# An attention and mLSTM kernel: the mLSTM chunks shared out over twelve attention items, queries split in the projection, output weights in another load order

## The chip, the cores and the metric

The kernel runs on one core of one Trainium2 chip. The metric is the device time of one execution in microseconds (us). A core has five engines that work in parallel: PE (matrix products), DVE (vector), ACT (scalar functions), POOL (a second, slower vector engine) and SP, whose queue here issues the DMA transfers. Each engine runs its own queue in order and waits for others through semaphores.

## The reference

One layer on 1024 tokens of width 1024, with 256 context tokens. One input projection feeds two head groups side by side; their outputs are concatenated, projected by w_out, and a feed-forward part follows.

```python
px = modulate(rms_norm(x, g_pre_mix), sh_m, sc_m) @ w_in
aq, ak, av, mq, mk, mv, mo, mg = split(px)
# 8 query heads on 2 key heads of 64, window 128, all 256 context keys, one sink logit per head
att = window_attention(rope(aq), rope(ak), av, kc, vc, attn_sink)
# 4 heads, keys of 64, values of 128, forward and backward scan, summed
h   = mlstm_bidir(mq, mk, mv, gates, state_f, state_b)
ml  = rms_norm(h) * gain * sigmoid(mo)
x   = x + gt_m * rms_norm(concat(att, ml) @ w_out)
x   = x + gt_f * rms_norm(swiglu(modulate(rms_norm(x), ...)))
```

Everything is float32. Where PE multiplies, an operand is split into a rounded part h and a remainder l (h by an ACT cast or a POOL multiplication, l by a subtraction), and products are summed from the parts: two for the scores (`qh`, `ql`), three for weights (`mm3`).

## The kernel before

The program goes through these stages, each with the time at which it stands in the profiled execution: modulation vectors and the token preparation (to about 150); the transposed projections (to 308), one tile of 128 output columns after the other in the order of `TILES`; attention with mLSTM (309 to 488); the output projection, the norms and the feed-forward part (to 1245). The change touches the second and third.

*Projection.* Each of the four query tiles `aq0` to `aq3` holds two heads. `rope` (L466-475) rotates the tile in the SBUF buffer `T(0)`, and two DMAs store it to the DRAM tensor `aq_d` (L616). After `aq3` come the tiles `mo0` to `mo3`, the sigmoid output gates (`so`, L620). Beside them the mLSTM queries are weighted: `ml_queries` loads weights into `qb` (L577), POOL multiplies (L580), and a store puts them into `q_dr` (L581).

*Attention.* There are 16 items, one per block of 128 queries and key group: item i is block i // 2, group i % 2, four heads. For an item `q_load` (L561) fetches `qd` from `aq_d`, and `q_split` makes `qh` and `ql` on POOL (L567, L568). `Soft` computes the scores of a head on PE (L774, L775: four matmuls in inner blocks, "one head" below), adds mask and minimum on DVE (L776), takes the exponential on ACT (L785) and normalizes on POOL (L790). `Values` transposes the probabilities on PE (`tr`, L804, "T"), splits them on ACT and DVE (L59, L60: `th`, `tl`), multiplies with the values (`mm`, L814, L815, "M") and combines the heads (`out`, L822, L823). Item i does its own values and the scores of item i + 2.

*mLSTM.* There are eight chunks n of 128 tokens, both directions. `ml_load` fetches weights `wl`, queries `qp` and gates `hs`; `ml_scores` (PE L689) puts scores into one of the two PSUM buffers called `s`, which the attention scores use too, and DVE multiplies them into `wl` (L694, four instructions); `ml_values` is called for four quarters of a chunk (PE L703, L704; DVE L707-709, L715; ACT L713); `ml_norm` squares on ACT (L722-724) and scales on POOL (L725); `ml_out` transposes on PE (L731, "z" with the chunk's number: z6 is the output of chunk 6) and multiplies with the gate on DVE (L732). Chunk i goes with item i, items 0 to 7; its output is taken one item later.

*Output weights.* `wout_load(j)` fetches 128 rows of w_out as `wor` (L744), casts to `woh` on ACT (L745) and subtracts to `wol` on POOL (L746); one j goes through half-wide loads with an ACT cast and a DVE subtraction instead (`load_split`). The three buffers are SBUF slots `R(k)`, shared in time with `wl`, `qp` and `hs`: a slot is written when its last reader is done. It runs in items 9 to 13.

*Order.* The instructions of a stage are put into their queues by a scheduler that works from the order in which the code calls them; `PLAN_ML` and `PLAN` are strings of operations that set this order for an item (T, M, O values; A scores and N norm of the item two ahead; q split; V, x, s, z, w mLSTM; l weights). The last two items, with the first block's output projection (`omm`: PE L71-73 on `woh`, `wol` and the split `mix`), are written out by hand behind `tc.manual_schedule()`.

Of the kernel before, what the change touches and what calls it, by code (L numbers as in the profile page):

```python
# [9 lines left out]
F32 = mybir.dt.float32  # L10
F32R = mybir.dt.float32r
# [20 lines left out]
VSIL, VCONV, VGML, VBADA, VGPM, VGPF = 0, 16, 28, 32, 64, 72  # L32
NVEC = 80
RW = 1032
PLAN_ML = "T0 q A0 A1 A2 A3 T1 T2 T3 M0 M1 T4 V0 N0 M2 V1 M3 M4 O z V2 w V3 s N1 x"
PLAN = "T0 q A0 A1 A2 A3 T1 T2 T3 N0 M0 T4 M1 M2 N1 M3 M4 O z l"


def body(tc, x, ctx, vecs, bcv, bada, gqm, gqf, wada, ws1, ws2, wt, wout, wfi, wfo,
# [45 lines left out]
    c = cp[1]  # L85
# [324 lines left out]
    dma(cost, cosc)  # L410
    dma(sint, sinc)
    so_d = tc.dram_tile([4, P, S], F32, name="so_d")
    aq_d = tc.dram_tile([8, 64, S], F32, name="aq_d")

    def T(i, name):
        return q2.tile([P, S], F32, name=name, tag=f"s{i}")
# [146 lines left out]
    def q_split(i):
        qd = qds.pop(i)
        qh = qq.tile([P, 4, P], F32R, name="qh", tag="qh", bufs=2)
        ql = qq.tile([P, 4, P], F32R, name="ql", tag="ql", bufs=2)
        pool.tensor_scalar(qh, qd, 1.0, 1.0, MUL, MUL)  # L567
        pool.tensor_tensor(ql, qd, qh.bitcast(F32), SUB)  # L568
        qhl[i] = qh, ql

    def ml_queries(d, j):

# [13 lines left out]
    for j, name in enumerate(TILES):  # L586
        if j + 1 < len(TILES):
            tload(j + 1)
        if name in rest2:
            ada_rest2(rest2[name])  # L590
        ps = tproj(j, name in ("mk0", "mk1", "ak"))
        i = int(name[-1]) if name[-1].isdigit() else 0
        if name.startswith("mk"):
            conv(ps, convw[:, 2 + i], (mk[i], mkc[:, i]), 1.0)
        elif name.startswith("mq"):
            conv(ps, convw[:, i], (mq[i],), 0.125)
        elif name == "ak":
            kr, ks = R(6, "kr", (S,)), R(7, "ks", (S,))
            rope(ps, kr, 1.0)
            kc = q2.tile([P, S + 2], F32, name="kc", tag="cr")  # L600
            act.copy(kc[:, 0:L], ps[2][:, :L])
            th = T(0, "kth")
            for a, b, w, dst in ((kr, ks, S, slice(0, S)), (kc[:, 0:L], kc[:, L:2 * L], L, slice(S, S + L))):
                t = th[64:P] if w == S else kc[64:P, 2 * L:3 * L]
                dma(b[0:64], a[64:P])
                dma(b[64:P], a[0:64])
                for g in range(2):
                    act.copy(k2[g][0:64, dst], (b if g else a)[0:64])
                    lo = (a if g else b)[64:P]
                    act.copy(t.bitcast(F32R), lo)  # L610
                    dve.tensor_tensor(k2[g][64:P, dst], lo, t, SUB)
        elif name.startswith("aq"):
            t = T(0, f"aq{i}")
            rope(ps, t, 0.125)
            for g in range(2):
                dma(aq_d[4 * g + i], t[64 * g:64 * g + 64])  # L616
        else:
            t = R(14 if i == 3 else 15, "so", (S,))
            for k in range(2):
                act.activation(t[:, k * 512:(k + 1) * 512], ps[k], AF.Sigmoid)  # L620
            dve.tensor_scalar(t, t, vec[:, VGML + i:VGML + 1 + i], None, MUL)
            dma(so_d[i], t)
        if name in rest:
            ada_rest(rest[name], j + 1)
        if name == "aq3":
            close(p2)
            aqp = open_pool("attq")
            qq = aqp[1]
            for i in range(2):
                q_load(i)  # L630
                q_split(i)
# [37 lines left out]
    wts, qps, hss = {}, {}, {}  # L669

    def ml_load(n):
        wts[n] = R((10, 12, 14)[n % 3], f"wl{n}", (2, 4, P))
        dma(wts[n].rearrange("p d h t -> p (d h t)"), w_dr[n])
        qps[n] = R((13, 15)[n % 2], f"qp{n}", (2, 2, P))
        for d in range(2):
            m = 7 - n if d else n
            dma(qps[n][:, d], q_dr[d, :, :, m * P:(m + 1) * P].rearrange("j p t -> p j t"))
        t = R((9, 11)[n % 2], f"hs{n}", (2, 4, P))
        dma(t[:, 1], so_d[:, :, n * P:(n + 1) * P].rearrange("h p t -> p h t"))
        hss[n] = t[:, 0], t[:, 1]  # L680
# [51 lines left out]
        dve.tensor_tensor(mix[n][:, 4:8, :], pt, so, MUL)  # L732

    def wout_load(j):
        h, l = R(2 * j, f"woh{j}", (D,), F32R), R(2 * j + 1, f"wol{j}", (D,), F32R)
        if j == 0:
            for i in range(2):
                sl = slice(i * 512, (i + 1) * 512)
                load_split(h[:, sl], l[:, sl], wout[j][:, sl],
                           qq.tile([P, 4, P], F32, name="wor0", tag="qd", bufs=2).rearrange("p a b -> p (a b)"))  # L740
            wo[j] = h, l
            return
        raw = R(2 * j - 1, f"wor{j}", (D,))
        dma(raw, wout[j])  # L744
        act.copy(h, raw)  # L745
        pool.tensor_tensor(l, raw, h.bitcast(F32), SUB)  # L746
# [77 lines left out]

    tc.keep_in_program_order(act.preload_act_table_set("natural_log_exp_and_others"))
    ml_load(0)
    for i in range(2):
        a = Soft(i)
        for h in range(4):
            a.scores(h)  # L830
            if h % 2:
                a.norm(h // 2)
        if i == 0:
            q_load(2)
            ml_scores(0)

    for i in range(NIT):
        a = Soft(i + 2) if i + 2 < NIT else None
# [2 lines left out]
            q_load(i + 3)  # L841
        if i == NIT - 2:
            break
        for k in (PLAN_ML if i < NT else PLAN).split():
            op, n = k[0], int(k[1:] or 0)
            if op == "q" and a:
                q_split(i + 2)
            elif op == "w" and i + 1 < NT:
                ml_load(i + 1)
            elif op == "T" and n < b.nt:  # L850
                b.tr(n)
            elif op == "M" and n < b.nt:
                b.mm(n)
            elif op == "O":
                b.out()
            elif op == "A" and a:
                a.scores(n)
            elif op == "N" and a:
                a.norm(n)
            elif op == "V" and i < NT:  # L860
                ml_values(i, n // 2, n % 2)
            elif op == "x" and i < NT:
                ml_norm(i)
            elif op == "s" and i + 1 < NT:
                ml_scores(i + 1)
            elif op == "z" and 1 <= i <= NT:
                ml_out(i - 1)
            elif op == "l" and i > NT:
                for j in {9: (7,), 10: (6,), 11: (5, 4), 12: (3, 2), 13: (1, 0)}[i]:
                    wout_load(j)  # L870
# [5 lines left out]
    mhl = {}  # L876

    def msplit(n, hf):
        h, l = (qq.tile([P, 4, P], F32R, name=f"m{x_}{hf}", tag=f"q{x_}", bufs=2) for x_ in "hl")
        split(h, l, mix[n][:, 4 * hf:4 * hf + 4, :])  # L880
        mhl[n, hf] = h, l

    def omm(n, hf, ks):
        h, l = mhl[n, hf]
        for k in ks:
            j = 4 * hf + k
            for i in range(2):
# [6 lines left out]

    b.tr(0)
    b.tr(1)
    msplit(0, 1)
    b.tr(2)
    omm(0, 1, range(1))
    mm_t(b, 0, 1)  # L900
    b.tr(3)
    omm(0, 1, range(1, 2))
    mm_t(b, 2, 3)
    b2 = Values(NIT - 1)
    b2.tr(0)
# [12 lines left out]
    close(atp)
    close(aqp)
# [787 lines left out]
```

## Time and profile before

| | us |
|---|---|
| median of 3 runs | 1248.03 (1245.07 to 1248.34) |
| profiled execution | 1247.24 |
| its span | 1245.4 |
| PE busy in the span | 1205.8 |
| DVE / ACT / POOL busy | 799.9 / 580.1 / 204.0 |

The granted TensorE clock is at its full value nearly throughout. In the page's fourth part, the chain that ended last, a step "DVE" or "DMA" means that the work behind it waited for that engine. The rows that matter for the change are those of the stage from 309 to 488.

### The profile page before, as it was taken

How to read it: one execution, taken by the hardware profiler on the slowest of the kernel's cores; microseconds unless marked ns; L12 is line 12 of the kernel's file. 1: busy time of each engine (PE TensorE's matmuls, PEld its weight loads, DVE VectorE, ACT ScalarE, POOL GpSimd, SP SyncE). 2: the span in 40 equal slices, each digit the busy share in tenths (PEclk: the TensorE clock that was granted, in tenths of full speed). 3: DMA queues.
4: the chain of work that ended last, by engine and by line, in shares of the span. 5: the costliest groups of instructions: out<-in, count | busy, mean ns of one | idle time of the engine just before them, and what ended most of it. 6: DMA issues, size and time to landing. Idle time of an engine off the chain costs nothing.

```text
span 1245.4 us, 16232 instructions
## 1 busy us (share of the span) xinstructions
PE 1205.8 (97%) x5859; PEld 971.7 (78%) x5859; DVE 799.9 (64%) x1375; ACT 580.1 (47%) x1111; POOL 204.0 (16%) x245
## 2 busy tenths in 40 slices
PE   7889999999999998999899999999999999999997
PEld 1779887877777786888678888888888878888885
DVE  3882268763877787355867677767776655554566
ACT  3754533111666796677633333333333325434542
POOL 0752401244644475000000000000000000000000
PEclk9899999999999999999999999999999999999999
DMA  8532855655422320522033465665644547665853
GB/s 310 173 123 73 300 164 152 186 147 197 121 85 86 114 74 9 203 81 72 17 104 140 162 220 189 216 237 191 216 144 169 180 160 268 203 212 187 308 172 118
DMA packets 90952, 201.78 MB, mean 162 GB/s; under 512 B 9076, under 2 KB 29940, under 8 KB 89464
## 3 DMA queue, kind: packets, MB, share of 16 engines
q1 hardware_dynamic: 90872, 200.74, 48.1%
q8 instruction: 46, 0.75, 0.2%
q14 instruction: 34, 0.28, 0.1%
HBM read 149.32 MB, written 50.73 MB: 161 GB/s over the span
## 4 chain that ended last, share of the span: by engine, by line
PE 74%; DVE 9%; DMA 7%; ACT 4%; POOL 2%; issue 2%; SPq 1%; DVEq 0%; POOLq 0%; ACTq 0%
PE xv L72 7%; PE xv L71 7%; PE xv L73 7%; PE pt L72 5%; PE pt L71 5%; PE pt L73 5%; PE pt L704 2%; PE pt L703 2%; PE pt L804 2%; DMA wb<-in_wada 2%; PE t L438 2%; PE t L441 2%; PE t L439 2%; PE s L774 1%; PE op L71 1%
## 5 line engine op out<-in xcount | busy, mean ns | idle before, releaser
L60 DVE TENSOR_TENSOR fo<-fr,fo 128x1024 fp32r<-128x1024 f32 x77 | 92.7, 1222 | 71.4 <-ACT fo L59 68.4
L59 ACT CAST fo<-fr 128x1024 fp32r<-128x1024 f32 x77 | 79.6, 1051 | 74.0 <-PE pt L73 36.5
L438 PE MATMUL t<-hh,th 128*128 128x512 f32 x208 | 83.4, 401 | 0.9 <-ACT cr L455 0.9
L439 PE MATMUL t<-hl,th 128*128 128x512 f32 x208 | 82.6, 397 | 0.0
L59 ACT CAST wS<-wr 128x512 fp32r<-128x512 f32 x88 | 54.1, 622 | 57.9 <-PE pt L73 38.0
L60 DVE TENSOR_TENSOR wS<-wr,wS 128x512 fp32r<-128x512 f32 x88 | 60.4, 688 | 20.8 <-ACT wS L59 20.7
L71 PE MATMUL xv<-tT,wS 128*128 128x512 f32 x168 | 67.7, 403 | 3.7 <-ACT tT L1079 2.0
L441 PE MATMUL t<-hh,tl 128*128 128x512 f32 x208 | 68.6, 394 | 0.0
L72 PE MATMUL xv<-tT,wS 128*128 128x512 f32 x168 | 67.6, 402 | 0.0
L73 PE MATMUL xv<-tT,wS 128*128 128x512 f32 x168 | 66.6, 397 | 0.3 <-DVE wS L60 0.3
L489 DVE SCALAR_TENSOR_TENSOR acc<-wb,csil,acc 128x1024 f32<-128x1024 f32 x24 | 34.4, 1433 | 39.4 <-DMA wb<-in_wada 39.2
L438 PEld LDWEIGHTS t<-hh,th 128*128 128x128 f32 x208 | 39.1, 188 | 10.1 <-ACT cr L455 1.3
L940 DVE TENSOR_TENSOR wr<-wr 128x512 f32<-128x512 f32 x66 | 45.5, 689 | 1.5
L439 PEld LDWEIGHTS t<-hl,th 128*128 128x128 f32 x208 | 39.1, 188 | 8.4 <-issue 1.2
L1191 ACT ACTIVATE es<-es 128x512 f32<-128x512 f32 x22 | 13.9, 632 | 67.6 <-DVE es L943 67.6
L441 PEld LDWEIGHTS t<-hh,tl 128*128 128x128 f32 x208 | 38.2, 188 | 8.5 <-issue 1.0
L71 PE MATMUL op<-woh,mh 128*128 128x512 f32 x112 | 44.7, 399 | 0.0
L72 PE MATMUL op<-wol,mh 128*128 128x512 f32 x112 | 44.2, 394 | 0.0
L73 PE MATMUL op<-woh,ml 128*128 128x512 f32 x112 | 44.1, 394 | 0.0
L774 PE MATMUL s<-k,qh 128*128 128x256 f32 (+1 forms) x128 | 41.5, 335 | 1.9 <-ACT so L620 1.0
L71 PE MATMUL pt<-fo 128*128 128x512 f32 x110 | 42.8, 389 | 0.0
L72 PE MATMUL pt<-fo 128*128 128x512 f32 x110 | 42.8, 389 | 0.0
(982 smaller groups left out, 3498.1 us busy)
## 6 DMA issues: line engine op xcount, KB each, us to landing
wr<-in_wfi SPq DMA_DIRECT2D x44, 512.0 KB, 5.0
wb<-in_wada SPq DMA_DIRECT2D x24, 512.0 KB, 4.1
s_d<-a SPq DMA_DIRECT2D x22, 512.0 KB, 6.5
bt<-in_wfo SPq DMA_DIRECT2D x44, 256.0 KB, 4.0
tb_d<-bt SPq DMA_DIRECT2D x11, 1024.0 KB, 3.9
fr<-s_d SPq DMA_DIRECT2D x44, 256.0 KB, 3.5
fr<-tb_d SPq DMA_DIRECT2D x44, 256.0 KB, 4.6
fr<-a_d SPq DMA_DIRECT2D x33, 256.0 KB, 4.3
```

What stands on the lines that cost most here:

```text
L59: act.copy(hi, raw)
L60: dve.tensor_tensor(lo, raw, hi.bitcast(F32), SUB)
L71: pe.matmul(ps, a[0], b[0], start=first, stop=False, **kw)
L72: pe.matmul(ps, a[0], b[1], start=False, stop=False, **kw)
L73: pe.matmul(ps, a[1], b[0], start=False, stop=last, **kw)
L438: pe.matmul(o, wh[:, kt], m[0], start=f, stop=False)
L439: pe.matmul(o, wh[:, kt], m[1], start=False, stop=False)
L441: pe.matmul(o, wl[:, kt], m[0], start=False, stop=l)
L489: dve.scalar_tensor_tensor(a, t, csil[:, kt, 0:1], a, MUL, ADD)
L703: pe.matmul(pv[:, j, :], qp_[r, d, j, :], cs[r, j, :], start=True, stop=False)
L774: pe.matmul(o, qh[:, h, :], k2[g][:, kc], start=True, stop=False)
L940: dve.tensor_tensor(out, a, b, SUB)
```

## The change

Three things are done at once.

1. *Queries.* `q_split` is gone. Each `aq` tile is split when it is projected (an ACT cast into slot 3, a DVE subtraction in place, 128 x 1024 each), and both parts are stored, so that `aq_d` becomes two DRAM tensors. The stores go from 8 to 16 (256 KB each) and the query loads of the items from 32 to 64 (128 KB each). The query tiles get three buffers in place of two.
2. *mLSTM.* One `PLAN` serves all items. At five places of an item, `a` to `e`, the table `ML3` names what is done of the mLSTM: three items do two chunks, so that eight chunks take twelve items (0 to 11, and the last output in item 12). In an entry the letter is the step (V values, s scores, x norm, y output, w and h loads), the first digit the chunk, counted from the first of the pair, and V's second digit the quarter. `ml_load` is cut in two.
3. *Output weights.* They are loaded in the order 1, 2, 3, 4, 0, 5, 6, 7 in place of 7, 6, 5, 4, 3, 2, 1, 0, in other slots (`WSLOT`, `WRAW`: the raw rows of 4, 0 and 5 share slot 14), and block 0's output projection begins with the attention half.

```diff
-PLAN_ML = "T0 q A0 A1 A2 A3 T1 T2 T3 M0 M1 T4 V0 N0 M2 V1 M3 M4 O z V2 w V3 s N1 x"
-PLAN = "T0 q A0 A1 A2 A3 T1 T2 T3 N0 M0 T4 M1 M2 N1 M3 M4 O z l"
+PLAN = "A0 A1 A2 A3 T0 T1 T2 T3 M0 M1 T4 a N0 M2 b M3 M4 O c d N1 e"
+ML3 = ({"a": "V00", "b": "V01", "c": "y9", "d": "V02", "e": "s1"},
+       {"a": "V03 x0", "b": "V10", "c": "V11", "d": "y0", "e": "w2 h2"},
+       {"a": "V12", "b": "s2", "c": "V13", "d": "", "e": "x1 w3"})
+WLOADS = {9: (1,), 10: (2, 3), 11: (4,), 12: (0, 5), 13: (6, 7)}
+WSLOT = ((0, 3), (1, 2), (4, 5), (6, 7), (8, 9), (10, 13), (14, 11), (12, 15))
+WRAW = (14, 8, 8, 8, 14, 14, 12, None)
...
-    def q_split(i):
-        qd = qds.pop(i)
-        qh = qq.tile([P, 4, P], F32R, name="qh", tag="qh", bufs=2)
-        ql = qq.tile([P, 4, P], F32R, name="ql", tag="ql", bufs=2)
-        pool.tensor_scalar(qh, qd, 1.0, 1.0, MUL, MUL)
-        pool.tensor_tensor(ql, qd, qh.bitcast(F32), SUB)
-        qhl[i] = qh, ql
+        qhl[i] = [qq.tile([P, 4, P], F32R, name=f"q{p}", tag=f"q{p}", bufs=3) for p in "hl"]
+        for t, src in zip(qhl[i], aq_d):
+            for d in range(2):
+                dma(t[64 * d:64 * d + 64].bitcast(F32), src[4 * g:4 * g + 4, :, n * P:(n + 1) * P].rearrange("h d t -> d h t"))
...
             rope(ps, t, 0.125)
-            for g in range(2):
-                dma(aq_d[4 * g + i], t[64 * g:64 * g + 64])
+            qp2 = R(3, f"aqh{i}", (S,), F32R), t.bitcast(F32R)
+            split(*qp2, t)
+            for d, o in zip(aq_d, qp2):
+                for g in range(2):
+                    dma(d[4 * g + i], o[64 * g:64 * g + 64].bitcast(F32))
...
+    def ml_work(i, k):
+        c0 = i // 3 * 2
+        for w in ML3[i % 3][k].split():
+            op, n, k_ = w[0], c0 + (int(w[1]) if w[1] != "9" else -1), int(w[2:] or 0)
...
-        h, l = R(2 * j, f"woh{j}", (D,), F32R), R(2 * j + 1, f"wol{j}", (D,), F32R)
+        h, l = (R(k, f"wo{p}{j}", (D,), F32R) for k, p in zip(WSLOT[j], "hl"))
...
+            raw = R(WRAW[j], f"wor{j}", (D,))
...
+    OORD = {0: (2, 3, 1, 0, 4, 5, 6, 7)}
```

How this moves instructions, at three places. First SP's queue at the end of the query tiles. Before, in order: the last query tile's stores, the loads of two items, the weights of the mLSTM queries (`qb`), with the third item's loads between.

```order
L616 DMA aq_d<-aq_2272 64x1024 x2
L561 DMA qd<-aq_d 64x4x128 x4
L577 DMA qb_2311<-w_d 64x8x128 x2
L577 DMA qb_2323<-w_d 64x8x128 x2
L561 DMA qd<-aq_d 64x4x128
L622 DMA so_d<-so 128x1024
L561 DMA qd<-aq_d 64x4x128 x3
L581 DMA q_dr<-qb_2311 128x1024
L577 DMA qb_2419<-w_d 64x8x128 x2
L581 DMA q_dr<-qb_2323 128x1024
L577 DMA qb_2514<-w_d 64x8x128 x2
```

The changed order at the same place:

```order
L619 DMA aq_dh<-aqh_2298 64x1024 x2
L619 DMA aq_dl<-aq_2288 64x1024 x2
L569 DMA qh<-aq_dh 64x4x128 x2
L569 DMA ql<-aq_dl 64x4x128 x2
L569 DMA qh<-aq_dh 64x4x128 x2
L569 DMA ql<-aq_dl 64x4x128 x2
L577 DMA qb_2330<-w_d 64x8x128 x2
L577 DMA qb_2342<-w_d 64x8x128 x2
L625 DMA so_d<-so 128x1024
L569 DMA qh<-aq_dh 64x4x128 x2
L569 DMA ql<-aq_dl 64x4x128 x2
L581 DMA q_dr<-qb_2330 128x1024
```

There are two more stores and four more query loads ahead of the first `qb` load.

Second PE's queue where a chunk's scores (`s<-mq,mk`) stand. Before, here the scores of chunk 5 in item 4; `pt<-cst,pr_` are transposes of probabilities:

```order
L704 MATMUL pt<-V,wl_3446 128x129
L689 MATMUL s<-mq_1333,mk_1331 128x128 x2
L689 MATMUL s<-mq_1334,mk_1332 128x128 x2
L774 MATMUL s<-k_0_1324,qh 128x384
L775 MATMUL s<-k_0_1324,ql 128x384
L774 MATMUL s<-k_0_1324,qh 128x256
L775 MATMUL s<-k_0_1324,ql 128x256
L804 MATMUL pt<-cst,pr__3309 128x128 x12
L814 MATMUL po<-th__3683,av_88 128x512
L774 MATMUL s<-k_0_1324,qh 128x384
L775 MATMUL s<-k_0_1324,ql 128x384
```

The changed order, here the scores of chunk 6 in item 8; `pt<-cst,hs_` is the output of chunk 4:

```order
L710 MATMUL pt<-V,wl_3712 128x129
L695 MATMUL s<-mq_1333,mk_1331 128x128 x2
L695 MATMUL s<-mq_1334,mk_1332 128x128 x2
L779 MATMUL s<-k_1_1325,qh 128x384
L780 MATMUL s<-k_1_1325,ql 128x384
L779 MATMUL s<-k_1_1325,qh 128x256
L780 MATMUL s<-k_1_1325,ql 128x256
L779 MATMUL s<-k_1_1325,qh 128x384
L780 MATMUL s<-k_1_1325,ql 128x384
L779 MATMUL s<-k_1_1325,qh 128x256
L780 MATMUL s<-k_1_1325,ql 128x256
L737 MATMUL pt<-cst,hs_3565 128x128 x4
```

The twelve transposes that stood between the first and the second head behind the chunk's scores now stand behind both heads and the output of chunk 4.

Third POOL's queue over the last items. Before (`pr_` are probabilities being normalized, `wol` the weights' remainders, here those of 4, 3, 2 and 1):

```order
L746 TENSOR_TENSOR wol_4635<-wor_4636,woh_4634 128x1024
L790 TENSOR_SCALAR pr__4416<-pr__4416,sm 128x640 x2
L567 TENSOR_SCALAR qh<-qd 128x512
L746 TENSOR_TENSOR wol_4744<-wor_4745,woh_4743 128x1024
L790 TENSOR_SCALAR pr__4525<-pr__4525,sm 128x640 x2
L763 COPY pr__4640<-bcr 128x4
L568 TENSOR_TENSOR ql<-qd,qh 128x512
L790 TENSOR_SCALAR pr__4525<-pr__4525,sm 128x640 x2
L746 TENSOR_TENSOR wol_4750<-wor_4751,woh_4749 128x1024
L763 COPY pr__4755<-bcr 128x4
L790 TENSOR_SCALAR pr__4640<-pr__4640,sm 128x512 x4
L746 TENSOR_TENSOR wol_4856<-wor_4857,woh_4855 128x1024
```

The changed order from the second last chunk output on; `hs_4027` is chunk 6, `hs_4304` chunk 7, and the `wol` are those of 4, 0, 5 and 6:

```order
L731 TENSOR_TENSOR hs_4027<-hs_4027,sq 128x512
L795 TENSOR_SCALAR pr__4502<-pr__4502,sm 128x640 x2
L751 TENSOR_TENSOR wol_4639<-wor_4640,woh_4638 128x1024
L768 COPY pr__4644<-bcr 128x4
L795 TENSOR_SCALAR pr__4644<-pr__4644,sm 128x512 x2
L751 TENSOR_TENSOR wol_4753<-wor_4754,woh_4752 128x1024
L795 TENSOR_SCALAR pr__4644<-pr__4644,sm 128x512 x2
L768 COPY pr__4764<-bcr 128x4
L751 TENSOR_TENSOR wol_4759<-wor_4760,woh_4758 128x1024
L731 TENSOR_TENSOR hs_4304<-hs_4304,sq 128x512
L795 TENSOR_SCALAR pr__4764<-pr__4764,sm 128x512 x4
L751 TENSOR_TENSOR wol_4861<-wor_4862,woh_4860 128x1024
```

The splits (`qh`, `ql`) are gone, and the scaling of chunk 7 stands behind the remainders of weights 4, 0 and 5. On PE the output of chunk 7 stands ahead of all transposes of item 13.

More of the change, by code (lines that the diff above doesn't have):

```diff
@@ L412, in body @@
     so_d = tc.dram_tile([4, P, S], F32, name="so_d")
-    aq_d = tc.dram_tile([8, 64, S], F32, name="aq_d")
+    aq_d = [tc.dram_tile([8, 64, S], F32, name=f"aq_d{p}") for p in "hl"]
     def T(i, name):
@@ L734, in wout_load @@
     def wout_load(j):
-        h, l = R(2 * j, f"woh{j}", (D,), F32R), R(2 * j + 1, f"wol{j}", (D,), F32R)
-        if j == 0:
-            for i in range(2):
+        h, l = (R(k, f"wo{p}{j}", (D,), F32R) for k, p in zip(WSLOT[j], "hl"))
+        if j == 7:
+            for i, p in enumerate("hl"):
                 sl = slice(i * 512, (i + 1) * 512)
                 load_split(h[:, sl], l[:, sl], wout[j][:, sl],
[L740 to L746, printed above, removed]
+                           qq.tile([P, 4, P], F32, name="wor7", tag=f"q{p}", bufs=3).rearrange("p a b -> p (a b)"))
+        else:
+            raw = R(WRAW[j], f"wor{j}", (D,))
+            dma(raw, wout[j])
+            act.copy(h, raw)
+            pool.tensor_tensor(l, raw, h.bitcast(F32), SUB)
         wo[j] = h, l
@@ L835, in body @@
             ml_scores(0)
+            ml_load(1)
+            ml_load2(1)
+    def ml_work(i, k):
+        c0 = i // 3 * 2
+        for w in ML3[i % 3][k].split():
+            op, n, k_ = w[0], c0 + (int(w[1]) if w[1] != "9" else -1), int(w[2:] or 0)
+            if not 0 <= n < NT:
+                continue
+            if op == "V":
+                ml_values(n, k_ // 2, k_ % 2)
+            elif op == "x":
+                ml_norm(n)
+            elif op == "y":
+                ml_out(n)
+                if w[1] == "9" and n + 2 < NT:
+                    ml_load2(n + 2)
+            elif op == "s":
+                ml_scores(n)
+            elif op == "w":
+                ml_load(n)
+            elif op == "h":
+                ml_load2(n)
     for i in range(NIT):
@@ L843, in body @@
             break
-        for k in (PLAN_ML if i < NT else PLAN).split():
+        for k in PLAN.split():
             op, n = k[0], int(k[1:] or 0)
[L846 to L850, printed above, removed]
+            if op == "T" and n < b.nt:
                 b.tr(n)
@@ L859, in body @@
                 a.norm(n)
[L860 to L870, printed above, removed]
+            elif op in "abcde":
+                ml_work(i, op)
+        for j in WLOADS.get(i, ()):
+            wout_load(j)
     order = tc.manual_schedule()
@@ L896, in body @@
     b.tr(1)
-    msplit(0, 1)
+    msplit(0, 0)
     b.tr(2)
-    omm(0, 1, range(1))
+    omm(0, 0, range(1))
     mm_t(b, 0, 1)
     b.tr(3)
-    omm(0, 1, range(1, 2))
+    omm(0, 0, range(1, 2))
     mm_t(b, 2, 3)
```

23 lines of the change are left out of this document (11 added, 12 removed).

## The prediction

> **What bounds the kernel now.** I read the page's shares and its chain first, then the span cut into stretches, then each engine in order of time where PE idles.
>
> ```profile
> PE 1205.8 (97%) x5859; PEld 971.7 (78%) x5859; DVE 799.9 (64%) x1375; ACT 580.1 (47%) x1111; POOL 204.0 (16%) x245
> ...
> PE 74%; DVE 9%; DMA 7%; ACT 4%; POOL 2%; issue 2%; SPq 1%; DVEq 0%; POOLq 0%; ACTq 0%
> ...
> 325.00:440.00 115.00, 113.90 (x675) 89.48 (x675) 86.10 (x282) 76.70 (x217) 54.59 (x71) 1.00 0.33 99
> 440.00:487.00 47.00, 42.19 (x269) 35.04 (x267) 42.69 (x94) 39.73 (x90) 38.36 (x39) 1.00 0.10 30
> ...
> 460.00:470.00 10.00, 9.88 (x67) 8.61 (x66) 9.91 (x25) 8.22 (x18) 10.00 (x11) 1.00 0.09 29
> 470.00:480.00 10.00, 8.61 (x59) 7.06 (x57) 8.52 (x22) 9.54 (x23) 10.00 (x12) 1.00 0.09 26
> 480.00:490.00 10.00, 7.13 (x35) 5.12 (x36) 8.62 (x13) 5.41 (x11) 3.47 (x5) 1.00 0.00 1
> ...
> 485.26 0.50 PE L815 MATMUL po<-tl__4820,av 128*128 128x512 f32 x1 [1.25 <-DVE tl__4820 L60]
> ```
>
> A stretch's row gives its length, then busy time and instructions of PE, its weight loads, DVE, ACT and POOL, then the granted clock; the last row is one instruction: start, duration, and the wait in front of it with its releaser. PE is busy for 97% of the whole. The stage that the change rewrites runs from 309.5 to 487.6, and PE fills its first part too (113.90 of 115). Only items 8 to 15 leave something: 4.81 us idle of 47, while POOL works without a pause (10.00 of 10) and DVE nearly so. So the change can win little, and PE waits that it makes weigh in full.
>
> The idle time is less than the loss, since matmuls that stand alone look long. I price the same 269 matmuls by their pitch where nothing waits:
>
> ```profile
> L774 PE MATMUL s<-k,qh 128*128 128x256 f32 (+1 forms) x36 | 11.0, 322 | 0.1
> ...
> 383.18 0.40 PE L815 MATMUL po<-tl__3540,av 128*128 128x512 f32 x1
> 383.41 0.60 PE L804 MATMUL pt<-cst,pr__3128 128*128 128x128 f32 x4
> ...
> 388.36 0.34 PE L774 MATMUL s<-k,qh 128*128 128x384 f32 x1
> ...
> 388.94 0.34 PE L774 MATMUL s<-k,qh 128*128 128x384 f32 x1
> ...
> 390.30 0.49 PE L703 MATMUL pt<-cs,qp 64*128 64x129 f32 x2
> ...
> 393.64 0.72 PE L689 MATMUL s<-mq,mk 64*128 64x128 f32 x8
> 394.28 0.45 PE L774 MATMUL s<-k,qh 128*128 128x384 f32 x1
> ...
> 394.97 1.47 PE L804 MATMUL pt<-cst,pr__3309 128*128 128x128 f32 x12
> 396.32 0.50 PE L814 MATMUL po<-th__3683,av 128*128 128x512 f32 x1
> 396.88 0.41 PE L774 MATMUL s<-k,qh 128*128 128x384 f32 x1
> ```
>
> One score head (four matmuls) takes 388.94 - 388.36 = 0.58 us; twelve transposes 396.32 - 394.97 = 1.35, or 0.1125 each; one value matmul 0.23 to 0.24 (383.18 to 383.41); two quarters of an mLSTM chunk's values 393.64 - 390.30 = 3.34. From 440 to 487 stand 72 score matmuls (L774's 36 and L775's 36), 132 transposes and, for the rest, some 61 value matmuls: 10.4 + 14.9 + 14.6 + 0.5 = 40.4 us. The loss there is about 6.6 us, which is 0.5% of the kernel.
>
> **Splits off POOL.** In each item two POOL instructions go:
>
> ```profile
> L568 POOL TENSOR_TENSOR ql<-qd,qh 128x512 fp32r<-128x512 f32 x14 | 18.0, 1286 | 0.8
> L746 POOL TENSOR_TENSOR wol<-wor,woh 128x1024 fp32r<-128x1024 f32 x7 | 17.0, 2430 | 0.7 <-PE pt L703 0.7
> ...
> L567 POOL TENSOR_SCALAR qh<-qd 128x512 fp32r<-128x512 f32 x14 | 8.7, 623 | 29.2 <-PE s L774 26.4 <-PE pt L704 2.8
> L725 POOL TENSOR_TENSOR hs<-hs,sq 128x512 f32<-128x512 f32 x8 | 8.3, 1041 | 20.2 <-ACT sq L724 20.2
> L745 ACT CAST woh<-wor 128x1024 fp32r<-128x1024 f32 x7 | 7.3, 1044 | 2.6 <-DMA wor<-in_wout 2.6
> ```
>
> These are 18.0 + 8.7 = 26.7 us of POOL in this stage. Up to 440 POOL has room (54.59 of 115), so they are worth something in two places. At the start:
>
> ```profile
> 313.63 1.27 POOL L568 TENSOR_TENSOR ql<-qd,qh 128x512 fp32r<-128x512 f32 x1
> 314.88 2.71 POOL L790 TENSOR_SCALAR pr__2708<-pr__2708,sm 128x512 f32<-128x512 f32 x4
> ...
> 315.63 0.55 PE L804 MATMUL pt<-cst,pr__2708 128*128 128x128 f32 x3 [0.34 <-POOL pr__2708 L790]
> ```
>
> The first normalization stood behind item 2's split, and PE's first transposes waited for it. It can start about a microsecond earlier; PE idled 0.34 in front of it and then followed POOL's pace, so I take -0.7 (ends 0 and -1.1). And in the tail, where the 6.6 us are lost: I count them all as taken back, -6.6 (least gain 0, if the waits are those of DVE and ACT and not POOL's), and then charge every new wait by name below.
>
> **The same splits in the projection.** Four ACT casts, four DVE subtractions of 128x1024, eight more stores, later 32 more loads:
>
> ```profile
> L60 DVE TENSOR_TENSOR fo<-fr,fo 128x1024 fp32r<-128x1024 f32 x77 | 92.7, 1222 | 71.4 <-ACT fo L59 68.4
> L59 ACT CAST fo<-fr 128x1024 fp32r<-128x1024 f32 x77 | 79.6, 1051 | 74.0 <-PE pt L73 36.5
> ...
> 259.74 1.29 DVE L472 SCALAR_TENSOR_TENSOR aq<-t,cost 128x512 f32<-128x512 f32 x2 [0.93 <-DMA aq_d<-aq]
> ...
> 230.00:300.00 70.00, 70.00 (x363) 54.31 (x362) 42.27 (x65) 11.80 (x18) 27.44 (x41) 1.00 0.59 175
> ```
>
> 4 x 1.22 us of DVE and 4 x 1.05 of ACT lie beside PE's matmuls. A query tile's buffer now comes free 2.3 us later (cast, subtraction, then its store), and the next rope already waits for that store by 0.93. From 230 to 300 PE is never idle while DVE has 28 us to spare of 70, so the rope's slack covers it: cost 0; if that fails once, at most 2.3. The added stores and loads stand on SP ahead of the mLSTM query loads (qb):
>
> ```profile
> 278.44 6.75 POOL L580 TENSOR_TENSOR qb<-qb,mq 128x128 f32<-128x128 f32 x16 [0.77 <-DMA qb<-w_d]
> ...
> 304.37 0.19 POOL L763 COPY pr__2708<-bcr 128x4 f32<-128x4 f32 x1 [2.82 <-DMA q_dr<-qb]
> ...
> 309.49 0.36 PE L774 MATMUL s<-k,qh 128*128 128x256 f32 x1 [1.03 <-ACT so L620]
> ```
>
> They come perhaps 3 us later, while PE's first score waits for ACT's last output-gate tile until 309.49. In exchange POOL loses two splits ahead of qb (2 x 1.9 us). Cost 0, ends -0.5 and +2.
>
> **Chunk scores between attention scores.** Both use the same two PSUM buffers. A row of before shows the price: scores of a chunk at 393.64, a head at 394.28, and the next head at 396.88, directly behind DVE's multiplications:
>
> ```profile
> 395.33 1.40 DVE L694 TENSOR_TENSOR wl<-wl,s 128x256 f32<-128x256 f32 x4
> ```
>
> They end at 396.73. Before, twelve transposes and a value matmul covered that wait. In three items (chunks 2, 4, 6) the changed order puts two heads directly behind the chunk's scores. If DVE is free, the second head starts 0.3 + 1.40 + 0.15 us after the chunk's scores end, against 0.6 for the head ahead of it: 1.2 us each, +3.6. Ends: 0 (the wait finds cover) and 7.8 (2.6 each, the distance from 394.28 to 396.88).
>
> **The sixth chunk's output (z6).** From its last values to z6 PE has two heads, two quarters of values, two more heads and five value matmuls, 1.2 + 3.3 + 1.2 + 1.2 = 6.9 us by the pitches above. In that time ACT must take squares and a root and POOL normalize (1.04), with two probability instructions of item 13 ahead of it. No row shows this order; I take half of the longest wait in the tail (1.25 at 485.26): +0.6, ends 0 and 1.3.
>
> **The last chunk's output (z7) and the weights.** In the changed order POOL does wol4, wol0 and wol5 ahead of the last chunk's normalization. Their raw weights share one slot, so each load waits for the subtraction before; wol4's slot is that of the sixth chunk's numbers, free only after z6. z7 stands on PE ahead of all of item 13's transposes.
>
> ```profile
> DMA to landing us min/median/max: 3.4/3.9/4.7
> ...
> 390.76 0.69 DVE L732 TENSOR_TENSOR mix<-pt,hs 128x512 f32<-128x512 f32 x1
> ...
> 480.71 2.76 POOL L790 TENSOR_SCALAR pr__4755<-pr__4755,sm 128x512 f32<-128x512 f32 x4
> ```
>
> From z6's start: its transposes and DVE's product 1.4; wol4 2.43 (3.8); load 3.9 (7.7); cast 1.04, wol0 2.43 (11.2); load 3.9 (15.1); cast 1.04, wol5 2.43 (18.6); normalization 1.04 (19.6). PE's work from z6 to z7, counted in the order: 40 transposes 4.5, 20 value matmuls 4.8, two quarters of values 3.35, 24 score matmuls 3.5, z6 0.5: 16.6. PE waits 3.0. Behind that, item 15's probabilities 2.76, wol6 2.43 and two half casts of wout's last rows (some 1.2 by the whole one) stand ahead of ACT's next casts of transposed probabilities: first output matmul at about 27.7, against 19.6 + 6.5 of PE work. Another 1.5. Together +4.5; ends 0 (if the chain starts 5 us earlier than I set it) and 8 (both loads at 4.7, DVE's product behind two score sums, 1.9).
>
> **Output weights in another order.** The matmuls and their number stay; block 0 merely begins with the other half. 0.
>
> **Sum.** -0.7 - 6.6 + 3.6 + 0.6 + 3.0 + 1.5 = +1.4 us on the profiled execution, 1247.24, so 1248.6; the median of the runs shown (1248.03) is 0.8 above that execution, and I put the forecast between: 1249.0.
>
> [...] How the clock answers to a thin PE shows at the start of the stage:
>
> ```profile
> 310.00:311.00 1.00, 0.67 (x6) 0.47 (x4) 0.79 (x2) 0.65 (x1) 0.00 (x0) 1.00 0.94 385
> ...
> 313.00:314.00 1.00, 1.00 (x9) 0.91 (x8) 0.83 (x3) 0.76 (x3) 0.92 (x2) 0.50 0.60 170
> ```
>
> PE's wait up to 309.49 and a use of 0.67 at 310 were followed by a granted clock of 0.50; behind the pause of 1.25 us at 485.26 the stretch's row keeps 1.00, so the sum charges nothing for z7's wait of 3.0. [...]
>
> **Rivals.**
> - *The new waits are hidden* (faster). For it: DVE is less loaded in the items of the chunk scores, since no item holds a whole chunk any more, and wol4 may start before I think. Then -7.3 plus the 1.5 behind the weights: -5.8, about 1242. Against it: DVE is 9.91 of 10 busy at 460 already, and the slots fix the chain. It decides if z7's wait is under 1 us and the chunk scores' waits under 0.4 each.
> - *The weights' chain before z7 is longer* (slower). Each microsecond by which wol4 starts late comes out on PE, one for one. If DVE's product behind z6 queues behind two score sums (1.9) and PE's wait of 4.9 then also brings the half clock as at 313 (1.7), the total is +1.4 + 1.9 + 1.7 = +5.0, about 1253. It decides from 2.3 us over my chain.
> - *The relief is worth nothing* (no change). PE's named waits at the end of the tail are on DVE's subtractions, as at 485.26, not on POOL. If the relief only moves the start and the new waits are half hidden, the result is between -1 and +3. It can't be told from the forecast by the time.
> - *The projection is delayed* by the query tile's buffer: +2 to +4 on top; little for it, with PE full there and DVE waiting.
>
> **How the numbers follow.** About 0.3%, 3.7 us, is what a measurement of this kernel can tell from no change. The forecast has 0.37 and the third rival 0.10, both "same": 0.47. The first rival has 0.25, the second 0.25 and the fourth 0.03: slower 0.28. The range leaves out a little on both sides: down to 1242.5, near the first rival's value, and up to 1254, just above the second's; the likeliest case's own range is 1245 to 1251.5.
>
> **What would show it.** Right: POOL no longer full from 460 to 480; a PE gap of 1 to 2 us in front of the second head behind chunk scores in three items; a gap of about 3 us in front of the last L737 of the changed code with POOL as releaser; first output matmul within 3 us of 487.6; nothing different from there on. Wrong: no gap at z7; PE busy under 10 of 10 in the projection; a first score later than 309.5 by over 1 us; or a difference behind 505.

## The result: slower by 0.9%

| | before | after |
|---|---|---|
| median of 6 runs | 1247.51 (1245.07 to 1249.96) | 1259.16 (1254.99 to 1263.76) |
| ratio to before | | 1.0092, 95% interval 1.0072 to 1.0112 |
| profiled execution | 1247.24 | 1254.99 |
| first score to first output matmul, profiled | 309.49 to 487.63: 178.14 | 308.86 to 495.02: 186.16 |
| from there to the end of the span | 757.8 | 758.2 |

The forecast was 1249.0, in a range of 1242.5 to 1254.0. In the profiled executions the whole loss lies in the stage that was rewritten: its start moved by 0.6 us, what follows it by 0.4. Inside it PE's busy time goes from 170.9 us to 172.3 and its idle time from 7.3 to 13.8, so most of the loss is waiting. The head of the page after:

```profile
span 1253.2 us, 16271 instructions
...
PE 1206.3 (96%) x5859; PEld 971.8 (78%) x5859; DVE 801.4 (64%) x1379; ACT 585.1 (47%) x1115; POOL 173.7 (14%) x213
...
PE 64%; DVE 6%; ACT 3%; issue 1%; POOL 1%; DMA 1%; DVEq 0%; ACTq 0%
```

POOL lost 30 us of work (204.0 to 173.7) and PE does the same matmuls; PE alone got later. The stage cut into stretches, two rows of before and then four of after (length, busy time of PE, its loads, DVE, ACT, POOL, granted clock):

```profile
340.00:380.00 40.00, 39.48 (x237) 31.04 (x237) 29.70 (x101) 24.55 (x72) 19.48 (x25) 1.00 0.28 81
380.00:440.00 60.00, 59.42 (x348) 46.76 (x347) 44.70 (x140) 42.91 (x117) 25.19 (x33) 1.00 0.37 116
```

```profile
340.00:380.00 40.00, 35.74 (x214) 28.73 (x212) 29.40 (x83) 25.50 (x71) 12.02 (x17) 0.96 0.28 76
380.00:440.00 60.00, 57.42 (x354) 45.40 (x353) 46.25 (x140) 39.76 (x107) 20.36 (x26) 1.00 0.37 104
440.00:487.00 47.00, 41.51 (x241) 31.85 (x240) 34.76 (x101) 36.34 (x96) 26.85 (x28) 1.00 0.31 90
487.00:505.00 18.00, 17.03 (x95) 14.15 (x93) 11.67 (x18) 10.43 (x19) 4.35 (x4) 0.92 0.00 1
```

From 340 to 440, where PE had idled 1.1 us, it idles 6.8. From 440 to 487, POOL fell from 38.36 to 26.85 and DVE from 42.69 to 34.76, and PE still idles 5.5 (4.8 before). PE's larger waits after, in order of time:

```profile
342.06 0.72 PE L695 MATMUL s<-mq,mk 64*128 64x128 f32 x8 [0.73 <-DVE sm L781]
...
344.47 0.41 PE L779 MATMUL s<-k,qh 128*128 128x384 f32 x1 [0.62 <-DVE sm L792]
...
347.13 1.11 PE L737 MATMUL pt<-cst,hs 128*128 128x128 f32 x4 [1.84 <-POOL hs L731]
348.04 2.49 PE L809 MATMUL pt<-cst,pr__2823 128*128 128x128 f32 x12
...
362.04 0.63 PE L809 MATMUL pt<-cst,pr__2956 128*128 128x128 f32 x4 [0.85 <-DVE tl__3295 L67]
...
384.36 0.72 PE L695 MATMUL s<-mq,mk 64*128 64x128 f32 x8
...
386.75 0.42 PE L779 MATMUL s<-k,qh 128*128 128x384 f32 x1 [0.90 <-DVE dn L715]
...
402.08 0.41 PE L779 MATMUL s<-k,qh 128*128 128x384 f32 x1 [0.29 <-DVE wl L700]
...
425.88 0.42 PE L779 MATMUL s<-k,qh 128*128 128x384 f32 x1 [0.90 <-DVE dn L715]
...
454.60 0.50 PE L819 MATMUL po<-th__4385,av 128*128 128x512 f32 x1 [0.76 <-ACT th__4385 L66]
...
466.34 0.66 PE L737 MATMUL pt<-cst,hs 128*128 128x128 f32 x4 [1.55 <-POOL hs L731]
...
486.38 0.92 PE L737 MATMUL pt<-cst,hs 128*128 128x128 f32 x4 [2.11 <-POOL hs L731]
...
495.02 0.50 PE L78 MATMUL s<-woh,mh 128*128 128x512 f32 x1 [0.50 <-ACT mh L66]
```

The L737 rows are the outputs z0, z6 and z7, each waiting for POOL's scaling. The rows at 386.75 and 425.88 are the second head behind the scores of chunk 4 (384.36) and of chunk 6 (423.49); DVE's multiplications (L700) end about 0.15 us before the named releaser does. Those at 362.04 and 402.08 stand behind the scores of chunks 3 and 5. The row at 348.04 matters most: twelve transposes stand directly behind z0, and take 2.49 us for what took 1.47 before. Why the scaling was late at z0, on POOL, and the root that it needs, on ACT:

```profile
342.24 1.58 POOL L795 TENSOR_SCALAR pr__3105<-pr__3105,sm 128x640 f32<-128x640 f32 x2 [3.85 <-DVE sm L792]
344.49 1.58 POOL L795 TENSOR_SCALAR pr__3105<-pr__3105,sm 128x640 f32<-128x640 f32 x2 [0.67 <-DVE sm L792]
346.04 1.04 POOL L731 TENSOR_TENSOR hs<-hs,sq 128x512 f32<-128x512 f32 x1
...
344.37 0.19 ACT L730 ACTIVATE sq<-sq 128x4 f32<-128x4 f32 x1
```

It is not POOL's load (it idled 3.85 and 0.67) but its order: the root is done at 344.56, and the scaling stands behind another item's probabilities, which had waited for DVE and end at 346.07. That is about 1.4 of the 1.84 us. The outputs z2 and z4 (387.41 and 426.54) stand at the same place on PE and wait for nothing: there POOL takes the scaling ahead of the second pair of probabilities, 0.1 us after the root. And the 2.49 us were taken at a granted clock of 0.50 (from 347 to 350), the 1.47 at 1.00. Around z0 and z7 in this trace (first three rows, then two), and, in a second trace of the same kernel, behind z0, z6 and z7:

```profile
340.00:346.00 6.00, 3.72 (x26) 2.94 (x24) 4.14 (x14) 4.16 (x18) 3.09 (x4) 1.00 0.31 89
346.00:350.00 4.00, 2.87 (x14) 2.87 (x15) 0.94 (x2) 0.60 (x2) 1.08 (x2) 0.59 0.00 0
350.00:354.00 4.00, 4.00 (x25) 3.12 (x24) 3.83 (x7) 2.84 (x5) 0.19 (x1) 0.99 0.22 66
...
484.00:486.00 2.00, 0.27 (x1) 0.00 (x0) 1.71 (x6) 1.98 (x6) 2.00 (x2) 1.00 0.00 0
486.00:490.00 4.00, 3.62 (x17) 3.52 (x18) 1.89 (x4) 2.62 (x6) 4.00 (x6) 0.58 0.00 0
```

```profile
348.00:352.00 4.00, 3.64 (x17) 3.62 (x18) 1.55 (x3) 1.17 (x2) 0.30 (x1) 0.57 0.11 32
...
466.00:470.00 4.00, 2.43 (x13) 2.24 (x12) 0.86 (x2) 1.45 (x6) 2.76 (x4) 0.73 0.03 12
470.00:474.00 4.00, 4.00 (x24) 3.38 (x23) 3.28 (x5) 2.79 (x5) 2.39 (x2) 0.84 0.18 38
...
488.00:492.00 4.00, 2.82 (x22) 2.35 (x22) 2.45 (x6) 3.59 (x8) 4.00 (x6) 1.00 0.00 0
```

Each low stretch costs 1.7 us of PE work by these rows (the length times one minus the granted clock), which is 3.4 us at the 0.50 granted from 347 to 350 and from 487 to 490. In the first trace one stands at z0 and one at z7 and none at z6; in the second at z0 and z6 and none at z7, with waits of the same size (z6 1.55 and 1.57, z7 2.11 and 2.10). Before has one, at 312, of 1.7 us too:

```profile
311.00:312.00 1.00, 0.84 (x5) 0.71 (x6) 0.77 (x4) 0.81 (x3) 0.00 (x0) 0.83 0.19 74
312.00:313.00 1.00, 1.00 (x6) 0.78 (x6) 0.76 (x2) 0.88 (x4) 0.07 (x1) 0.50 0.00 0
...
314.00:315.00 1.00, 1.00 (x6) 0.86 (x4) 0.75 (x3) 0.70 (x2) 1.00 (x2) 0.50 1.09 408
315.00:316.00 1.00, 0.66 (x6) 0.43 (x5) 1.00 (x5) 0.00 (x0) 1.00 (x2) 0.96 0.52 209
```

### The profile page after: what moved, and what is told of

It is laid out like the page before. It is cut to its first block, busy times and chain, and to the rows that moved or that the text cites. A ratio compares the mean times of both kernels' runs of the same rounds, so it can differ in the third digit from the quotient of the medians.

```text
span 1253.2 us, 16271 instructions
## 1 busy us (share of the span) xinstructions
PE 1206.3 (96%) x5859; PEld 971.8 (78%) x5859; DVE 801.4 (64%) x1379; ACT 585.1 (47%) x1115; POOL 173.7 (14%) x213
## 4 chain that ended last, share of the span: by engine, by line
PE 64%; DVE 6%; ACT 3%; issue 1%; POOL 1%; DMA 1%; DVEq 0%; ACTq 0%
PE xv L79 7%; PE xv L78 7%; PE xv L80 7%; PE pt L79 5%; PE pt L78 5%; PE pt L80 5%; PE pt L710 2%; PE pt L709 2%; PE pt L809 2%; PE op L79 1%; PE op L78 1%; PE op L80 1%; PE fx L78 1%; PE fx L80 1%; PE fx L79 1%; PE fy L78 1%
```

## The experiments

All times in the table are profiled, of one execution each: from the first score to the first output matmul, what of it went to half clock (in stretches of 2 us, the length times one minus the granted clock), the rest; then the median of the runs, the ratio to before with its interval, and the mean granted clock of the runs.

| kernel | stage | half clock | rest | median | ratio | clock |
|---|---|---|---|---|---|---|
| before | 178.1 | 1.7 | 176.4 | 1247.4 to 1248.0 | | 0.993 |
| after | 186.2 | 3.4 | 182.8 | 1259.16 | 1.0092 (1.0072 to 1.0112) | 0.988 |
| after, again | 186.7 | 3.4 | 183.3 | 1258.40 | 1.0084 (1.0069 to 1.0098) | 0.990 |
| e1: queries alone | 178.8 | 1.7 | 177.0 | 1247.74 | 1.0006 (0.9988 to 1.0023) | 0.992 |
| e2: queries, weights | 176.1 | 0 | 176.1 | 1247.23 | 0.9994 (0.9983 to 1.0005) | 0.992 |
| e3: chunks, weights | 189.6 | 5.1 | 184.5 | 1258.64 | 1.0086 (1.0068 to 1.0104) | 0.989 |
| e5: after, raw slot | 189.5 | 1.7 | 187.8 | 1260.95 | 1.0107 (1.0080 to 1.0135) | 0.988 |
| e11: after, z0 later | 186.6 | 6.8 | 179.8 | 1257.13 | 1.0076 (1.0058 to 1.0094) | 0.987 |
| e7: after, z0 z2 z4 later | 178.9 | 1.7 | 177.2 | 1249.63 | 1.0017 (1.0002 to 1.0032) | 0.991 |
| e4: z6 later too | 178.1 | 0 | 178.1 | 1250.18 | 1.0012 (0.9996 to 1.0028) | 0.992 |
| e6: e4, raw slot | 175.7 | 0 | 175.7 | 1247.17 | 0.9986 (0.9971 to 1.0000) | 0.992 |
| e9: e6, z7 by DVE | 179.5 | 3.4 | 176.1 | 1247.92 | 0.9999 (0.9987 to 1.0012) | 0.992 |
| e10: e9, casts on POOL | 174.0 | 0 | 174.0 | 1245.06 | 0.9981 (0.9967 to 0.9996) | 0.993 |
| e8: e2, casts on POOL | 174.8 | 0 | 174.8 | 1245.41 | 0.9978 (0.9963 to 0.9993) | 0.992 |

**Which part?** e1 is before with the first part alone, e2 adds the third, e3 is the changed kernel without the first. The first part's edit is that of the change; e3 puts it back:

```diff
-PLAN = "A0 A1 A2 A3 T0 T1 T2 T3 M0 M1 T4 a N0 M2 b M3 M4 O c d N1 e"
+PLAN = "q A0 A1 A2 A3 T0 T1 T2 T3 M0 M1 T4 a N0 M2 b M3 M4 O c d N1 e"
```

e1: 

> The kernel before with the first part alone: queries split in the projection and stored as two DRAM tensors, mLSTM and weights as before. Theory A (the loss lies in the places of the mLSTM steps: outputs z0, z6, z7 and chunk scores stand on PE ahead of work that could cover them): no loss here, the tail wins what POOL's splits cost, -2 to -6 us against before. Rival B (the loss lies in the queries' way through DRAM, more stores, 64 loads on SP): +5 us or more against before. Rival C (weights' order and slots): same as A here.

e2: 

> First and third part: queries split in the projection, weights in the new order and slots, mLSTM one chunk per item as before. Theory A: within 2 us of the first-part-only kernel, so 2 to 6 us under before, because without mLSTM in items 8 to 12 nothing waits for the weights' slots. Rival B: +5 or more against before. Rival C: 5 us or more over the first-part-only kernel.

e3: 

> The changed kernel without its first part: queries are split on POOL in the items again, one DRAM tensor, mLSTM over twelve items and weights in the new order. Theory A: as slow as the changed kernel or slower by up to 4 us (POOL has the splits as well), 1256 to 1264, with PE waits of 1.5 us and more in front of z0, z6 and z7. Rival B: within 3 us of before. Rival C: as A.

e1 and e2 can't be told from before, e3 not from the changed kernel; in e3's trace z0, z6 and z7 wait 1.90, 3.17 and 2.14. So the loss came with the mLSTM's new places, and neither the queries' way through DRAM (rival B) nor, without the new places, the weights' order (rival C) costs or brings anything that can be measured. No run has the new places with the old order of the weights, so what the two cost together, as in the chain before z7, is not separated. The gain that theory A expected of e1 did not come. From 440 to 487, e1 and then e2:

```profile
440.00:487.00 47.00, 42.44 (x268) 34.94 (x266) 42.20 (x95) 40.93 (x93) 33.84 (x33) 1.00 0.16 47
```

```profile
440.00:487.00 47.00, 43.58 (x266) 34.95 (x266) 43.18 (x94) 41.77 (x93) 24.87 (x29) 1.00 0.22 68
```

In e2 POOL has 13 us less than before (38.36) and PE idles 3.4 in place of 4.8. That POOL worked without a pause there was true, and it was not what PE waited for: DVE, at 43 of 47, is as full as it was.

**Which places?** e7 takes the outputs of chunks 0, 2 and 4 one item later, e11 that of chunk 0 alone (`i < 3`), e4 all four even ones:

```diff
+        late = {(1, "d"): "", (1, "e"): "w2", (2, "c"): "y0 h2 V13"}
-        for w in ML3[i % 3][k].split():
+        for w in (late if i < 9 else {}).get((i % 3, k), ML3[i % 3][k]).split():
```

e7: 

> The changed kernel, with the outputs of chunks 0, 2 and 4 taken one item later (from place d of the second item of three to place c of the third, with the gates' load behind them); the tail as it was. Theory D (the early loss is z0's wait of 1.84 us, the waits of 1.6 us around chunk 2's scores ahead of it and the half clock behind them, because there was no cover between scores and output): these go, no PE wait over 0.7 us from 320 to 355, 3 to 5 us under the changed kernel (about 1255). Rival E (the waits only move to the next place, since DVE and ACT are late anyway): within 1.5 us of the changed kernel.

e11: 

> The changed kernel with chunk 0's output alone taken one item later; chunks 2, 4 and 6 as changed. Theory D (most of the early loss is the place around 341 to 350: 3.9 us of PE idle and 0.85 of half clock): from the first score to the first output matmul 181 to 182 us against 186.2, and the other two moved outputs are worth 2 to 3 us. Rival H (each of the three outputs costs alike, by its place ahead of the transposes): 183 to 184 us.

e4: 

> The same for all four even chunks, so z6 too comes one item later; weight 4's subtraction, which waits for z6's slot, then starts later. Theory D: z6's wait of 1.55 us goes, but from z6 to z7 stand only about 10.5 us of PE work against 12 of the chain (product 1.4, wol4 2.4, load 3.9, cast 1.0, wol0 2.4, scaling 1.0): z7 waits 1.5 to 3; total within 2 us of the kernel with chunks 0, 2, 4 alone moved. Rival E: within 1.5 us of the changed kernel.

e7's ratio falls from 1.0092 to 1.0017: 9.5 us by the medians, twice what was expected. The place of z0 in e7, on PE, and its stretch in e7:

```profile
341.52 1.04 PE L809 MATMUL pt<-cst,pr__2823 128*128 128x128 f32 x8
342.49 0.71 PE L695 MATMUL s<-mq,mk 64*128 64x128 f32 x8
...
350.03 0.60 PE L737 MATMUL pt<-cst,hs 128*128 128x128 f32 x4
...
340.00:350.00 10.00, 9.71 (x64) 8.09 (x64) 8.89 (x25) 8.10 (x26) 4.30 (x6) 1.00 0.26 75
```

The transposes of item 2, the same that stood behind z0 at 348 in the changed kernel, are done from 341.5 on; z0 comes at 350.03 and waits for nothing. With z0 no longer at its old place, the scheduler also put these transposes around the chunk's scores, so the two costs went together, and the experiment doesn't separate them.

In the column "rest", e11 against after is -3.0 to -3.5 and e7 against e11 -2.6: z0's place is worth somewhat more than those of z2 and z4 together, as theory D has it; each figure is the difference of single traces. But the stage of e11 is no shorter than after's, against 181 to 182 forecast, and its runs are only 1 to 2 us faster, and the intervals don't tell them apart from the changed kernel's. In the trace the reason is a half-clock stretch of 10 us in the tail, 5.1 us of PE work; that its runs have the lowest mean clock of all, 0.987, fits. ACT, PE, and PE's stretch in e11:

```profile
450.56 1.04 ACT L750 CAST woh<-wor 128x1024 fp32r<-128x1024 f32 x1 [2.46 <-DMA wor<-in_wout]
```

```profile
452.43 0.50 PE L819 MATMUL po<-th__4385,av 128*128 128x512 f32 x1 [2.59 <-ACT th__4385 L66]
...
453.00:465.00 12.00, 11.85 (x38) 8.79 (x39) 6.88 (x22) 5.71 (x17) 2.83 (x4) 0.57 0.03 6
```

ACT stood at a weight's cast, waiting 2.46 for its load, with the transposed probabilities' cast behind it; PE waited 2.59, and in stretches of 2 us the granted clock is 0.67 from 454, 0.50 from 456 to 464 and 0.77 from 464. The same wait is 0.76 and 0.80 in the two traces of after. In e5 it is 2.57, in front of the same instruction and with the same work behind it, and the clock stays at 1.00 (440 to 487): a wait of this length had half clock behind it in one trace and not in the other. In e7 ACT idles for the load too (2.01), but PE waits only 0.61 and 0.20 there. That this is because chunks 2 and 4 moved, and thus the weights' place in time, is likely but was not tried alone.

Against e7, e4 gains z6's wait (1.56) and some of z7's (2.10 to 1.50), and pays at z5 (0.42), at the same ACT cast (0.95) and in front of the first output matmul (1.05): within its error the same as e7, as expected.

**The second trace of the changed kernel.**

> The changed kernel once more, for a second trace. Theory D: the same waits at z0, z6 and z7 in the same size; where the time differs from the first trace it differs by half-clock stretches behind these waits and by the DMA time up to the first score. Rival: other waits than in the first trace.

The waits are the same to 0.05 us (z0 1.84 and 1.84, z6 1.55 and 1.57, z7 2.11 and 2.10), and the half-clock stretches sit elsewhere. The two sets of six runs have mean clocks of 0.988 and 0.990, before 0.993: 0.003 to 0.005 of 1258 us, 4 to 6 us, against 1.7 us more in the traces. So of the 11 to 12 us, 6.4 to 6.9 are waits ("rest", from the traces) and the other 4 to 5, by this estimate, half clock. That it lies behind these waits in the other runs too is argued from the two traces and not shown.

**z7 and the weights.** e5 changes one number in the changed kernel, e6 the same in e4:

```diff
-WRAW = (14, 8, 8, 8, 14, 14, 12, None)
+WRAW = (10, 8, 8, 8, 14, 14, 12, None)
```

e5: 

> The changed kernel with one number changed: the raw rows of weight 0 go into slot 10 in place of slot 14, so that their load no longer waits for weight 4's subtraction, and weight 5's load waits for that of 4 alone. Theory A: z7's wait of 2.1 us falls under 0.7, the first output matmul comes 28.7 - 23 to 26 us behind z6, total 2 to 5 us under the changed kernel and with less spread from run to run, if the half clock behind z7's wait goes with it; still slower than before. Rival B: within 1 us of the changed kernel. Rival C: down to within 2 us of before.

e6: 

> The kernel with all even outputs later, and weight 0's raw rows in slot 10, so that their load waits for no subtraction. Theory D: the chain from z6 to z7 is about 7.3 us without a load in it; what is left at z7 is ACT's queue; z7's wait under 1.5 us; 1 to 4 us under the same kernel without the slot change, about 1251 to 1254, still not under before. Rival E: no difference from it.

e5 went against theory A: z7's wait rose to 3.53. POOL and PE of e5:

```profile
489.85 1.36 POOL L795 TENSOR_SCALAR pr__4764<-pr__4764,sm 128x512 f32<-128x512 f32 x2 [1.51 <-DVE sm L792]
491.33 1.04 POOL L731 TENSOR_TENSOR hs<-hs,sq 128x512 f32<-128x512 f32 x1
...
492.43 1.05 PE L737 MATMUL pt<-cst,hs 128*128 128x128 f32 x4 [3.53 <-POOL hs L731]
```

With the load off the chain, wol5 is done early, at 488.34, and what holds the scaling is now half of item 15's probabilities, which the scheduler put ahead of it: they wait 1.51 for DVE and end at 491.21, and the scaling starts at 491.33. The wait is a new one in the old place. e6 is 3 us under e4, as expected, but at 1247.17 instead of 1251 to 1254, and not by the expected way: z7 still waits 1.76. Its trace lacks e4's ACT wait (0.95) and z5's (0.42); whether these are the slot's doing was not settled.

e9 takes the scaling of chunk 7 off POOL:

```diff
-        pool.tensor_tensor(hs, hs, hcast(sq), MUL)
+        (dve if n == NT - 1 else pool).tensor_tensor(hs, hs, hcast(sq), MUL)
```

> The kernel with all even outputs later and weight 0 in slot 10, and the scaling of chunk 7 done on DVE in place of POOL, so that no weight stands ahead of it. Theory I (z7's last wait of 1.76 us is POOL's queue): z7's wait under 0.6, 1 to 2 us under the parent, 1245 to 1246. Rival (it is ACT's queue in front of the root): z7's wait stays over 1.2, total as the parent.

ACT, DVE and PE of e9 at z7:

```profile
477.59 0.19 ACT L730 ACTIVATE sq<-sq 128x4 f32<-128x4 f32 x1
```

```profile
478.09 1.23 DVE L731 TENSOR_TENSOR hs<-hs,sq 128x512 f32<-128x512 f32 x1
...
479.47 0.63 PE L737 MATMUL pt<-cst,hs 128*128 128x128 f32 x4 [1.41 <-DVE hs L731]
```

The wait stays at 1.41: theory I falls. The root ends on ACT at 477.78, behind casts and exponentials; DVE then needs a score sum's end and 1.23 us for the scaling, which takes POOL 1.05 in the changed kernel (485.27), though in subtractions of 128x1024 POOL is the slower one (2.43 against DVE's 1.22 in before). The releaser's name was only the last link of the chain.

**Casts to POOL.** POOL now has room (24.87 of 47 busy from 440 to 487 in e2), so e8 moves the weights' casts (ACT) and the last one's subtraction (DVE) to it in e2, e10 the casts of weights 1, 2, 3 and 7 in e9:

```diff
-        act.copy(h, raw)
+        pool.tensor_scalar(h, raw, 1.0, 1.0, MUL, MUL)
         pool.tensor_tensor(l, raw, h.bitcast(F32), SUB)
```

e8: 

> The kernel with the first and third part (queries split in the projection, new weight order, mLSTM as before), and in addition all casts of the output weights (ACT, 1.04 us each) and the subtractions of the last one (DVE, 1.22 each) are done on POOL, which has room since the splits left it. Theory F (the 6.6 us lost in the tail of before are ACT's and DVE's, which is why taking POOL's splits away gained nothing): PE's loss from 440 to 487 falls by 2 to 4 us, total 2 to 4 under its parent, 1243 to 1245. Rival G (the tail's loss is latency between PE and DVE, not load): within 1 us of its parent.

e10: 

> The same, and POOL also casts weights 1, 2, 3 and 7 (from ACT) and subtracts weight 7 (from DVE). If ACT's and DVE's load in the tail still holds PE: 1 to 3 us under the kernel with chunk 7's scaling on DVE, 1243 to 1245, the fastest of all. If it is latency: within 1 us of that kernel.

Both are faster than before by 0.2%, with intervals just clear of 1, and can't be told from each other; against their parents the intervals overlap. So that the casts bring anything is not shown. PE's idle time in e8 from 440 to 487 is as in e2, so even if theory F's sign fits, its place doesn't:

```profile
440.00:487.00 47.00, 43.60 (x274) 36.04 (x273) 42.99 (x94) 38.83 (x89) 32.20 (x38) 1.00 0.22 68
```

With its outputs moved, another raw slot and casts on POOL, the shared-out mLSTM (e10) is 13 to 14 us under the changed kernel and 2.4 under before; the plan with one chunk per item gets as far (e8). So no run shows that sharing out the chunks brings anything by itself.

## Why the prediction was wrong, step by step

- *Splits off POOL, -6.6 in the tail.* This step failed, and it is the largest. POOL at 10.00 of 10 was read as the limit; e1 and e2 take the splits away and gain nothing (ratios 1.0006 and 0.9994, where 6.6 us would be 0.9947), and e3 puts them back into the changed kernel and loses nothing. The rows for the other reading were quoted (the waits there name DVE) and got the third rival's 0.10. Without this term the sum gives +8.0, and the profiled execution is 7.75 slower; that closeness is in part luck, since the terms below err both ways.
- *-0.7 at the start.* The wait of 0.34 for POOL is gone, but half clock at the start alone differs by more than that from trace to trace (1.7 us in before and e1, none in after, 3.4 in e9). Neither shown nor refuted.
- *Projection and queries, 0.* Right: e1 at 1.0006, with PE's first score at 308.31.
- *Chunk scores, +3.6.* Right in place and nearly in size: around chunk 2's scores the waits are 0.73, 0.22 and 0.62, behind those of chunks 4 and 6 0.90 each, 3.4 in all; the second heads alone have 2.4. Chunks 3, 5 and 7 were given nothing and have 0.85, 0.29 and 0.29.
- *Chunk outputs.* z6 was given 0.6 and waited 1.55. z0 was given nothing: it stands directly behind the two heads, as z4 does in the quoted order, and I priced the second head's wait and not the output's behind it. It waits 1.84, the largest early wait; z2 and z4 wait for nothing.
- *z7 and weights, +4.5.* The chain is right, its waits were put too high: z6 to z7 19.6 forecast, 20.04 measured; wait 3.0 and 2.11. From z7 to the first output matmul 8.1 were forecast and 8.64 measured, but that is luck: 1.7 of it is half clock, and the second trace, without half clock there, has 7.73.
- *Clock, 0.* Failed. The stage lost 3.4 us to half clock in each of the two traces of the changed kernel, against 1.7 before. The 1.7 that the second rival charges for one stretch is what before shows from 311 to 316, and each of the changed kernel's stretches has that size. The waits at which they stand are 1.57 to 2.11 us long, in thin PE work; at 313 in before PE had waited 1.03 and 0.49. z6 and z7 have one in one trace and none in the other, at the same waits; what decides that was not shown. I took the row at 485.26, a single pause without half clock, as enough to charge nothing for z7's.
- *The rivals.* The sign was the second rival's, its mechanism wasn't: the chain before z7 was as long as forecast.

## What to carry to other kernels

An engine that is busy without a pause need not be the limit: POOL was busy for 10.00 of 10 us, and without its splits e1 took 1.0006 of the time before. See whether the waits of the bounding engine name it, and even then take its load away in thought and ask whether those waits would end earlier: in e6 POOL was named at z7, and without POOL 1.41 of the 1.76 us stayed. When steps are moved in an in-order queue, price for each the work that stands between its last input and itself, and move late-input steps (here an output transposition) behind independent work that is ready. In this kernel z7's wait cost 2.11 us and, with the half clock at it, 1.7 more in one trace, and 2.10 alone in the other.

## What the runs showed of the hardware

In these traces the half clock came in stretches of 3.4 us (1.7 us lost) or of two or three times that: 6.8 us at the start of e9, around a wait of 2.05, and some 10 us in e11, behind one of 2.59. From 340 us on, each stands at or behind a wait of 1.5 us or more in thin PE work, but not every such wait has one (2.57 in e5: none). At the start of the stage before has one behind waits of 1.03 and 0.49, and the changed kernel has none behind 0.94 and 0.50. Of the changed kernel's six runs the slowest, 1263.76, had the lowest mean clock, 0.984; the fastest, 1254.99, had 0.991 and the run with 0.994 took 1256.91. The 0.007 between slowest and fastest are an estimated 8.8 of 1259 us, as much as the two differ, so by this estimate the clock is most of the scatter; the run with 0.994 shows that it is not all of it.
